# Binary cross-entropy over 8192 x 8192: three slots of predictions with one slot of 8-bit targets, in place of two slots of each

## Chip, cores and metric

The kernel runs on one core of one Trainium2 chip. The metric is the device time of one execution in microseconds (us); for the kernel before it is the median of three runs. Engines are named as in the profile: DVE is VectorE, ACT is ScalarE, POOL is GpSimd, SP is SyncE. DMA transfers are issued from the instruction queues of POOL, SP or ACT and are carried out by the core's 16 DMA engines.

## What is computed

For two float32 arrays of 8192 x 8192 the kernel returns a third of the same shape. `target` holds only 0.0 and 1.0.

```python
pred = np.clip(pred, eps, 1 - eps)          # eps = 1e-7
return -(target * np.log(pred) + (1 - target) * np.log(1 - pred))
```

As a target is 0 or 1, both kernels compute -ln|t - 1 + p|: that is -ln(p) for t = 1 and -ln(1 - p) for t = 0.

## The kernel before, in words

All arrays are read as flat lists. A chunk of w columns is a stretch of 128 x w numbers, and each of the 128 partitions holds w numbers of it that lie together in memory. The whole array is 524,288 columns, and a full chunk is 15,360 columns (60 KiB a partition in float32).

`plan` (L15) lays the chunks out: two halves of 7,680 columns, then 32 full chunks, then two halves and a last piece. `ring_p` (L58) holds predictions in float32, in two slots of 15,360 columns and a small one for the last piece. The result is written over the predictions in place and stored from there. `ring_t` (L59) has the same layout in bfloat16; the load of the targets converts from float32 on the way (L73). A small side piece of 32 rows and 1,408 columns goes through tiles of its own (`side_p`, `side_t`), with four loads or stores of 8 rows each on SP.

Each stretch passes five instructions:

- clip (L92, DVE): max and min with the two bounds
- merge (L95, DVE): (t - 1) + p, which reads the targets
- Abs and Ln (L98, L99, ACT)
- negate (L102, DVE): times -1

The order is written out by hand and each engine keeps it. In the main loop a chunk is worked in two halves of 7,680: clip and merge of the first half, clip and merge of the second, negate of the first, negate of the second. Then the store of the chunk is issued on POOL, and behind it on the same queue the target load and the prediction load of the chunk after next, which go into the same slot:

```python
        for k in range(2, n - 4):
            front(k, (0, 2))
            front(k, (1, 2))
            back(k, (0, 2))
            back(k, (1, 2))
            store(k)
            ...
            for j in range(k + 2, n if k == n - 5 else k + 3):
                load(j)
```

A target slot is free as soon as its merges are done. A prediction slot is free only when the store that reads it has landed, so POOL waits at each prediction load (L74) for the store that it has just issued. At the end the last full chunk is followed by two halves and the last piece, and the last three stores are on SP.

Of the kernel before, what the change touches and what calls it, by code (L numbers as in the profile page):

```python
# [1 line left out]

# [4 lines left out]

EPS = 1e-7

BIG = 15 * 1024  # L10
HALF = BIG // 2
SIDE = 1408


def plan(total):  # L15

    n, last = divmod(total, BIG)
    assert n > 4 and 0 < last <= 2048
    spots = [(HALF, 0), (HALF, HALF)]
    spots += [(BIG, k % 2 * BIG) for k in range(1, n - 1)]  # L20
    end = (n - 1) % 2 * BIG
    return spots + [(HALF, end), (HALF, end + HALF), (last - SIDE // 4, 2 * BIG)]

@with_exitstack
def kernel(
    ctx: ExitStack,
    tc: tile.TileContext,
    pred: bass.AP,  # L30
    target: bass.AP,
    out: bass.AP,
):
    nc = tc.nc
    fp32 = mybir.dt.float32
    bf16 = mybir.dt.bfloat16
    Alu = mybir.AluOpType
    Act = mybir.ActivationFunctionType
    P = nc.NUM_PARTITIONS

    R, C = pred.shape
    spots = plan(R * C // P)
    n = len(spots)
    widths = [w for w, _ in spots]
    turn = n // 2
    cut = R * C - sum(widths[:turn]) * P
    starts = [cut + sum(widths[:k]) * P for k in range(turn)]
    starts += [sum(widths[turn:k]) * P for k in range(turn, n)]

    def chunk(ap, k):  # L50
        flat = ap.rearrange("r c -> (r c)")
        return flat[starts[k] : starts[k] + widths[k] * P].rearrange("(p w) -> p w", p=P)

    pool = ctx.enter_context(tc.tile_pool(name="rings", bufs=1))
    ring = [P, 2 * BIG + widths[-1]]
    ring_p = pool.tile(ring, fp32, name="ring_p", tag="ring_p")
    ring_t = pool.tile(ring, bf16, name="ring_t", tag="ring_t")
    warm = pool.tile([1, 8], fp32, name="warm", tag="warm")  # L58
    side_p = pool.tile([32, SIDE], fp32, name="side_p", tag="side_p")  # L59
    side_t = pool.tile([32, SIDE], fp32, name="side_t", tag="side_t")  # L60

    def side(ap, j):
        flat = ap.rearrange("r c -> (r c)")
        return flat[cut - 32 * SIDE : cut].rearrange("(p w) -> p w", p=32)[j:32:4]

    def spot(ring, k, part=(0, 1)):
        w, c = spots[k]
        i, m = part
        return ring[:, c + i * w // m : c + (i + 1) * w // m]

    def load(k):
        queue = nc.sync if k == 0 else nc.gpsimd
        nc.gpsimd.dma_start(out=spot(ring_t, k), in_=chunk(target, k))  # L73
        queue.dma_start(out=spot(ring_p, k), in_=chunk(pred, k))  # L74

    def store(k):
        queue = nc.sync if k >= n - 3 else nc.gpsimd
        queue.dma_start(out=chunk(out, k), in_=spot(ring_p, k))  # L78

    def load_side():  # L80
        nc.vector.memset(side_p[:, 0:2], 0.5)  # L81
        nc.vector.memset(side_t[:, 0:2], 0.0)  # L82
        for j in range(4):
            nc.sync.dma_start(out=side_t[j:32:4, :], in_=side(target, j))
            nc.sync.dma_start(out=side_p[j:32:4, :], in_=side(pred, j))

    def store_side():
        for j in range(4):
            nc.sync.dma_start(out=side(out, j), in_=side_p[j:32:4, :])

    def front_of(p, t):
        nc.vector.tensor_scalar(  # L92
            out=p, in0=p, scalar1=EPS, scalar2=1 - EPS, op0=Alu.max, op1=Alu.min
        )
        nc.vector.scalar_tensor_tensor(  # L95
            out=p, in0=t, scalar=1.0, in1=p, op0=Alu.subtract, op1=Alu.add
        )
        nc.scalar.activation(out=p, in_=p, func=Act.Abs)  # L98
        nc.scalar.activation(out=p, in_=p, func=Act.Ln)  # L99

    def back_of(p):
        nc.vector.tensor_scalar(out=p, in0=p, scalar1=-1.0, scalar2=None, op0=Alu.mult)  # L102

    def front(k, *part):
        front_of(spot(ring_p, k, *part), spot(ring_t, k, *part))

    def back(k, *part):
        back_of(spot(ring_p, k, *part))

    with tc.manual_schedule():  # L110
        nc.vector.memset(warm, 1.0)  # L111
        for k in range(3):
            load(k)
        nc.scalar.activation(out=warm, in_=warm, func=Act.Ln)  # L114
        front(0)
        front(1)
        back(0)
        store(0)
        back(1)
        store(1)  # L120
        load(3)
        for k in range(2, n - 4):
            front(k, (0, 2))
            front(k, (1, 2))
            back(k, (0, 2))
            back(k, (1, 2))
            store(k)
            if k == n - 6:
                load_side()
            if k == n - 5:  # L130
                front_of(side_p, side_t)
            for j in range(k + 2, n if k == n - 5 else k + 3):
                load(j)
        z, a, b, c = range(n - 4, n)
        front(z, (0, 2))
        back_of(side_p)
        store_side()
        front(z, (1, 2))
        back(z, (0, 2))
        front(a)  # L140
        back(z, (1, 2))
        store(z)
        front(b, (0, 2))
        front(b, (1, 2))
        back(a)
        store(a)
        front(c)
        back(b)
        store(b)
        back(c)  # L150
        store(c)


# [1 line left out]
_INS = ['pred', 'target']  # L155
_OUTS = [((8192, 8192), 'float32')]


# [23 lines left out]
```

## Time and profile before

| what | value |
|---|---|
| runs | 1865.12, 1866.41, 1866.94 us; median 1866.41 |
| span of the profiled execution, first to last instruction | 1864.3 us |
| what lies around the span, against the median of the runs | 2.1 us |
| DVE busy | 1124.7 us (60%) |
| ACT busy | 902.1 us (48%) |
| POOL busy (its DMA issues) | 57.6 us (3%) |
| bytes at the SBUF side of the transfers | 671.22 MB |
| read from HBM, written to HBM | 536.87 MB, 268.44 MB |
| HBM traffic over the span | 432 GB/s |
| merge (L95), 128x7680 | 67 times, 8158 ns each |
| clip (L92) and negate (L102), 128x7680 | 67 and 68 times, 4157 and 4160 ns each |
| Abs (L98) and Ln (L99), 128x7680 | 67 times each, 6596 and 6602 ns |

The profile has no separate time for the execution that it shows: the span stands for it, and what lies around it is taken as the difference to the median. In the page, "busy" is the time in which an engine executes; waits for a semaphore are not in it. The DMA row gives the mean busy share of the 16 DMA engines in 40 slices, and the GB/s row under it counts bytes at the SBUF side, where a target counts 2 bytes before the change although 4 are read from HBM. In a row of the timeline the first two numbers are the start and the duration in us, and the brackets tell how long the engine had been idle and what ended that.

### The profile page before, as it was taken

The numbers are of one execution on the slowest core, as the hardware profiler recorded it, in microseconds if no ns is written. First come the engines' busy times: TensorE is split into PE (matmuls) and PEld (weight loads), VectorE is DVE, ScalarE is ACT, GpSimd is POOL, SyncE is SP. The second block draws the span as 40 slices with busy tenths as digits, with TensorE's granted clock in tenths as the row PEclk, the third lists the DMA queues.
The fourth block names the chain that finished last, engine by engine and source line by source line (L and its number), as shares of the span: only waits on it lengthen the run. The fifth ranks groups of instructions, "written<-read, shape, count | busy, mean of one in ns | idle before, by whom it ended". The sixth has DMA issues, their size and how long they took to land.

```text
span 1864.3 us, 649 instructions
## 1 busy us (share of the span) xinstructions
DVE 1124.7 (60%) x215; ACT 902.1 (48%) x144; POOL 57.6 (3%) x111
## 2 busy tenths in 40 slices
DVE  4655766555676655557665555766555576655585
ACT  3355553335555333555533355553335555333665
POOL 0000000000000000000000000000000000000000
DMA  9999999999999999999999999999999999999999
GB/s 295 376 357 340 357 339 370 386 380 355 341 355 343 369 388 379 356 341 355 349 364 388 380 355 343 353 353 360 389 378 355 349 348 353 359 388 384 347 341 385
DMA packets 16180, 671.22 MB, mean 360 GB/s; under 512 B 1872, under 2 KB 1872, under 8 KB 2352
## 3 DMA queue, kind: packets, MB, share of 16 engines
q0 software_dynamic: 15408, 657.98, 98.4%
q1 hardware_dynamic: 768, 13.21, 1.7%
q14 instruction: 4, 0.03, 0.0%
HBM read 536.87 MB, written 268.44 MB: 432 GB/s over the span
## 4 chain that ended last, share of the span: by engine, by line
DMA 35%; issue 26%; ACT 22%; DVE 15%; POOL 1%; DVEq 0%; POOLq 0%; PEldq 0%
DMA ring_p<-in_pred_dram 32%; ACT ring_p L98 11%; ACT ring_p L99 11%; DVE ring_p L95 7%; DVE ring_p L92 4%; DVE ring_p L102 4%; DMA out_dram<-ring_p 3%; POOL ring_t L73 0%; POOL out_dram L78 0%; DVEq L177 0%; POOL ring_p L74 0%; POOLq L78 0%; POOLq L73 0%; DVEq L92 0%; PEldq L177 0%
## 5 line engine op out<-in xcount | busy, mean ns | idle before, releaser
L98 ACT ACTIVATE ring_p<-ring_p 128x7680 f32<-128x7680 f32 (+1 forms) x70 | 450.3, 6433 | 933.4 <-DVE ring_p L95 933.4
L95 DVE SCALAR_TENSOR_TENSOR ring_p<-ring_t,ring_p 128x7680 f32<-128x7680 bf16 (+1 forms) x70 | 556.9, 7955 | 2.4
L92 DVE TENSOR_SCALAR ring_p<-ring_p 128x7680 f32<-128x7680 f32 (+1 forms) x70 | 283.8, 4055 | 397.9 <-DMA ring_p<-in_pred_dram 397.9
L102 DVE TENSOR_SCALAR ring_p<-ring_p 128x7680 f32<-128x7680 f32 (+1 forms) x69 | 283.8, 4114 | 321.2 <-ACT ring_p L99 321.2
L99 ACT ACTIVATE ring_p<-ring_p 128x7680 f32<-128x7680 f32 (+1 forms) x70 | 450.8, 6440 | 2.2
L74 POOL DMA_DIRECT2D ring_p<-in_pred_dram x36 | 19.3, 536 | 909.5 <-DMA out_dram<-ring_p 909.5
L78 POOL DMA_DIRECT2D out_dram<-ring_p x34 | 18.3, 539 | 852.0 <-DVE ring_p L102 827.7
L73 POOL DMA_DIRECT2D ring_t<-in_target_dram x37 | 20.3, 550 | 0.8 <-PEq L177 0.8
L98 ACT ACTIVATE side_p<-side_p 32x1408 f32<-32x1408 f32 x1 | 1.4, 1375 | 6.7 <-DVE side_p L95 6.7
L114 ACT ACT_TABLE_LOAD x1 | 1.3, 1283 | 0.7 <-PEq L166 0.7
L95 DVE SCALAR_TENSOR_TENSOR side_p<-side_t,side_p 32x1408 f32<-32x1408 f32 x1 | 1.6, 1611 | 0.0
L99 ACT ACTIVATE side_p<-side_p 32x1408 f32<-32x1408 f32 x1 | 1.4, 1375 | 0.0
L92 DVE TENSOR_SCALAR side_p<-side_p 32x1408 f32<-32x1408 f32 x1 | 0.9, 874 | 0.0
L102 DVE TENSOR_SCALAR side_p<-side_p 32x1408 f32<-32x1408 f32 x1 | 0.9, 873 | 0.0
L111 DVE MEMSET warm<- 1x8 f32 x1 | 0.1, 65 | 0.8 <-PEq L166 0.8
L114 ACT ACTIVATE warm<-warm 1x8 f32<-1x8 f32 x1 | 0.2, 208 | 0.0
L166 POOL MEMSET const-float32-0.0<- 128x1 f32 x1 | 0.1, 98 | 0.2 <-issue 0.2
L166 POOL MEMSET const-bfloat16-1.0<- 128x1 bf16 x1 | 0.1, 101 | 0.0
L166 POOL MEMSET const-uint8-127<- 128x1 uint8 x1 | 0.1, 99 | 0.0
L166 POOL MEMSET const-float32-1.0<- 128x1 f32 x1 | 0.1, 98 | 0.0
L81 DVE MEMSET side_p<- 32x2 f32 x1 | 0.1, 60 | 0.0
L82 DVE MEMSET side_t<- 32x2 f32 x1 | 0.1, 60 | 0.0
## 6 DMA issues: line engine op xcount, KB each, us to landing
ring_p<-in_pred_dram POOLq DMA_DIRECT2D x32, 7680.0 KB, 35.9
out_dram<-ring_p POOLq DMA_DIRECT2D x32, 7680.0 KB, 29.2
ring_t<-in_target_dram POOLq DMA_DIRECT2D x32, 3840.0 KB, 46.8
ring_p<-in_pred_dram POOLq DMA_DIRECT2D x3, 3840.0 KB, 35.7
ring_t<-in_target_dram POOLq DMA_DIRECT2D x4, 1920.0 KB, 28.2
out_dram<-ring_p POOLq DMA_DIRECT2D x2, 3840.0 KB, 28.1
out_dram<-ring_p SPq DMA_DIRECT2D x2, 3840.0 KB
ring_p<-in_pred_dram SPq DMA_DIRECT2D x1, 3840.0 KB
```

What stands on the lines that cost most here:

```text
L73: nc.gpsimd.dma_start(out=spot(ring_t, k), in_=chunk(target, k))
L74: queue.dma_start(out=spot(ring_p, k), in_=chunk(pred, k))
L78: queue.dma_start(out=chunk(out, k), in_=spot(ring_p, k))
L81: nc.vector.memset(side_p[:, 0:2], 0.5)
L82: nc.vector.memset(side_t[:, 0:2], 0.0)
L92: nc.vector.tensor_scalar(out=p, in0=p, scalar1=EPS, scalar2=1 - EPS, op0=Alu.max, op1=Alu.min)
L95: nc.vector.scalar_tensor_tensor(out=p, in0=t, scalar=1.0, in1=p, op0=Alu.subtract, op1=Alu.add)
L98: nc.scalar.activation(out=p, in_=p, func=Act.Abs)
L99: nc.scalar.activation(out=p, in_=p, func=Act.Ln)
L102: nc.vector.tensor_scalar(out=p, in0=p, scalar1=-1.0, scalar2=None, op0=Alu.mult)
L114: nc.scalar.activation(out=warm, in_=warm, func=Act.Ln)
L166: nc = _bacc.Bacc("TRN2", target_bir_lowering=False, num_devices=1)
```

## The change

- **Slots.** `ring_p` has three slots of 15,360 columns. `ring_t` has one slot of 15,360 columns in uint8, so the target load converts float32 to 8-bit integers and the merge reads 8-bit integers.
- **Chunks.** The first chunk has 5,120 columns, then come 33 full chunks, then a tail of 5,632, 5,632 and 1,024 columns that together lie in one slot. The stretches follow each other in memory from the start. The side piece and its tiles are gone.
- **Order on POOL.** In the loop: the target load of the next chunk (it waits for the merges of this chunk), the store of this chunk (it waits for the negates), the prediction load of the chunk after next (it waits for the store of the chunk before, whose slot it takes). The very first prediction load is on ACT's queue.
- **Order on DVE.** merge, merge, negate, negate of chunk k, then clip, clip of chunk k+1. Before, the clips came right ahead of the merges of their own chunk.
- **End.** The three tail predictions are loaded behind the store of chunk 32, the three tail targets behind the merges of chunk 33. DVE then has negate of the first half of chunk 33, the three tail clips, the first tail merge, and only then negate of the second half of chunk 33 and its store. The last four stores are on SP; the very last is cut into 108, 12 and 8 rows.

```diff
-    spots = [(HALF, 0), (HALF, HALF)]
-    spots += [(BIG, k % 2 * BIG) for k in range(1, n - 1)]
-    end = (n - 1) % 2 * BIG
-    return spots + [(HALF, end), (HALF, end + HALF), (last - SIDE // 4, 2 * BIG)]
+WIDE = 15360
+SLOTS = 3
+TAIL = (5632, 5632, 1024)
+ROWS = (108, 12, 8)
...
+    low = mybir.dt.uint8
...
+    spots = [(first, 0)]
+    spots += [(WIDE, k % SLOTS * WIDE) for k in range(1, n + 1)]
+    c = (n + 1) % SLOTS * WIDE
+    for w in TAIL:
+        spots.append((w, c))
+        c += w
...
-    ring_p = pool.tile(ring, fp32, name="ring_p", tag="ring_p")
-    ring_t = pool.tile(ring, bf16, name="ring_t", tag="ring_t")
+    ring_p = pool.tile([P, SLOTS * WIDE], fp32, name="ring_p", tag="ring_p")
+    ring_t = pool.tile([P, WIDE], low, name="ring_t", tag="ring_t")
...
-    def load(k):
-        queue = nc.sync if k == 0 else nc.gpsimd
-        nc.gpsimd.dma_start(out=spot(ring_t, k), in_=chunk(target, k))
-        queue.dma_start(out=spot(ring_p, k), in_=chunk(pred, k))
+    def load_p(k):
+        queue = nc.scalar if k == 0 else nc.gpsimd
+        queue.dma_start(out=p_of(k), in_=chunk(pred, k))
+
+    def load_t(k):
+        nc.gpsimd.dma_start(out=t_of(k), in_=chunk(target, k))
 
     def store(k):
-        queue = nc.sync if k >= n - 3 else nc.gpsimd
-        queue.dma_start(out=chunk(out, k), in_=spot(ring_p, k))
+        queue = nc.sync if k >= z else nc.gpsimd
+        r = 0
+        for rows in ROWS if k == n - 1 else (P,):
+            queue.dma_start(out=chunk(out, k)[r : r + rows, :], in_=p_of(k)[r : r + rows, :])
+            r += rows
...
+    halves = (0, 2), (1, 2)
+    tail = range(z + 1, n)
     with tc.manual_schedule():
+        load_p(0)
+        load_t(0)
+        load_p(1)
...
+        for h in halves:
+            clip(0, h)
+        for k in range(z):
+            for h in halves:
+                merge(k, h)
+            load_t(k + 1)
+            for h in halves:
+                negate(k, h)
+            for h in halves:
+                clip(k + 1, h)
             store(k)
+            for j in (k + 2,) if k + 2 <= z else tail if k + 2 == z + 1 else ():
+                load_p(j)
+        for h in halves:
+            merge(z, h)
+        for j in tail:
+            load_t(j)
+        negate(z, halves[0])
+        for j in tail:
+            clip(j)
+        merge(z + 1)
+        negate(z, halves[1])
         store(z)
+        merge(z + 2)
+        negate(z + 1)
+        store(z + 1)
+        merge(z + 3)
+        negate(z + 2)
+        store(z + 2)
+        negate(z + 3)
+        store(z + 3)
```

In the changed kernel `merge` holds the merge, Abs and Ln of a stretch, `clip` and `negate` one instruction each. z is 33, the last full chunk, and the tail is chunks 34, 35 and 36.

## The prediction

> **What bounds the kernel now.** I read the page first (busy shares, the DMA row, HBM bytes), then the timeline for the clips (each waits for a prediction load, so its start is a landing time), then one period of the loop, then the windows view.
>
> ```profile
> DVE 1124.7 (60%) x215; ACT 902.1 (48%) x144; POOL 57.6 (3%) x111
> ...
> DMA  9999999999999999999999999999999999999999
> ...
> HBM read 536.87 MB, written 268.44 MB: 432 GB/s over the span
> ```
>
> No engine is busy for more than 60%, while the DMA engines are in the top tenth in every slice. POOL's 909.5 us of waiting and ACT's 933.4 are waits of engines that have time. The kernel is as long as its transfers.
>
> ```profile
> 590.00:600.00 10.00, 8.62 (x2) 10.00 (x2) 0.00 (x0) 1.00 1.08 233
> ...
> 674.00:690.00 16.00, 11.40 (x2) 0.00 (x0) 0.00 (x0) 1.00 1.02 442
> ```
>
> The last two numbers are the DMA share and GB/s at the SBUF side. The first stretch is a target load, the second a prediction load. Both keep the DMA engines full, but the target load lands half as much a microsecond: the time goes by the 4 bytes read per number, not by the 2 that land.
>
> ```profile
> 40.29 4.16 DVE L92 TENSOR_SCALAR ring_p<-ring_p 128x7680 f32<-128x7680 f32 x1 [8.14 <-DMA ring_p<-in_pred_dram]
> ...
> 78.15 4.16 DVE L92 TENSOR_SCALAR ring_p<-ring_p 128x7680 f32<-128x7680 f32 x1 [8.04 <-DMA ring_p<-in_pred_dram]
> ...
> 406.83 4.16 DVE L92 TENSOR_SCALAR ring_p<-ring_p 128x7680 f32<-128x7680 f32 x1 [12.31 <-DMA ring_p<-in_pred_dram]
> ...
> 515.50 4.16 DVE L92 TENSOR_SCALAR ring_p<-ring_p 128x7680 f32<-128x7680 f32 x1 [11.38 <-DMA ring_p<-in_pred_dram]
> ...
> 1711.11 4.16 DVE L92 TENSOR_SCALAR ring_p<-ring_p 128x7680 f32<-128x7680 f32 x1 [11.42 <-DMA ring_p<-in_pred_dram]
> ```
>
> From 515.50 to 1711.11 lie 22 chunks of three transfers, 66 in all: **18.115 us for one transfer of 15,360 columns** (a unit). By 40.29 two units are through (four halves): 36.2 us of work, so the landing is 4.1 late. By 78.15 it is 4 units, late by 5.7; by 406.83 22 units, late by 8.3; by 515.50 28 units, again late by 8.3. So the lateness grows by 4.2 us in the first 400 us and then stands still. The views do not tell why it grows.
>
> **The change, part by part.** Bytes at HBM are the same: three times 524,288 columns, 102.4 units, 1855.0 us. What can change is the lateness, stalls in which no transfer is queued, and the end.
>
> *8-bit targets.* The load still reads 4 bytes per number. By the two window rows its time goes by those, so I cost it at 0. The trace shows no 8-bit load: as bounds, 2% less of a unit (more would contradict rows in which half the bytes landed brought nothing) is -0.36 x 33.3 targets = -12 us, and 2% more +12. The merge reads 8-bit where it read bfloat16. The rows have 1611 ns for 1,408 columns of float32 targets and 1926 for 1,696 of bfloat16: about 1.14 ns a column in both, so the type of the targets does not show, and I take 0. If it took twice as long, see the rivals.
>
> *The loop.* Call T the landing of targets k. The queue then holds store k-1, predictions k+1, targets k+1: busy until T + 54.3. Here are the distances from a merge to its store, before:
>
> ```profile
> 411.02 8.16 DVE L95 SCALAR_TENSOR_TENSOR ring_p<-ring_t,ring_p 128x7680 f32<-128x7680 bf16 x1
> ...
> 438.98 6.60 ACT L99 ACTIVATE ring_p<-ring_p 128x7680 f32<-128x7680 f32 x1
> 445.62 4.16 DVE L102 TENSOR_SCALAR ring_p<-ring_p 128x7680 f32<-128x7680 f32 x1 [8.97 <-ACT ring_p L99]
> 450.07 0.54 POOL L78 DMA_DIRECT2D out_dram<-ring_p  x1 [24.33 <-DVE ring_p L102]
> ```
>
> From the first merge to the store's issue it is 39.05 us; ACT's four passes make it, so a merge pair without a clip between changes nothing. In the changed loop the merges end at T + 16.4 and targets k+1 are issued then, 20 us before the queue reaches them (T + 36.2). Store k is issued at T + 39.05, 15 us before T + 54.3. Predictions k+2 wait for store k-1, landed at T + 18.1, and go out right behind store k. DVE needs 2 x 8.16 + 2 x 4.16 + 2 x 4.16 = 33.0 of 54.3 us. The single target slot is thus hidden by two queued transfers, and the loop stays at 54.35 us a chunk. Cost 0.
>
> *The first chunk is short*, and there the cover is thin. When targets 1 land (2.67 units), the queue holds store 0 (a third), predictions 2 and targets 2: until T + 42.3. Store 1 goes out at T + 39.05 and moves data 1.1 later (a store issued on POOL at 1819.64 shows in the windows from 1820: 241 GB/s, then 538), at T + 40.2. That is 2.1 us of cover. But clip 2 now starts on DVE 0.3 us before that issue, where before DVE waited at this place. One spot of the trace has a DVE clip over a POOL issue:
>
> ```profile
> 1753.98 0.87 DVE L92 TENSOR_SCALAR side_p<-side_p 32x1408 f32<-32x1408 f32 x1
> 1754.35 0.62 POOL L78 DMA_DIRECT2D out_dram<-ring_p  x1 [24.32 <-DVE ring_p L102]
> 1754.88 1.61 DVE L95 SCALAR_TENSOR_TENSOR side_p<-side_t,side_p 32x1408 f32<-32x1408 f32 x1
> 1754.97 0.55 POOL L73 DMA_DIRECT2D ring_t<-in_target_dram  x1
> ```
>
> The issue takes 0.62 us in place of 0.54 (mean 539 ns over 34) and ends 0.12 after the clip. I read it as: an issue under a clip is held until the clip ends. With a clip of 4.16 the data of store 1 start at T + 38.8 + 4.16 + 0.12 + 0.8 = T + 43.9, a stall of **1.6 us**, once. From below it is 0 (no hold), from above 5.8 (held through both clips). In the loop the same hold, at worst to T + 48.1, is covered by T + 54.3. The Trainium skill says the same of this spot (SBUF — State Buffer, section "SBUF: two separate sides"): while VectorE runs an operation that takes both ports, GpSimd cannot write the descriptors of the transfers that it issues. By that rule the sum is the forecast or up to 4.2 us above it; without it, 1.6 below. The 0.12 us agree with it, on one short row.
>
> *Lateness.* The same traffic, now each store between a target load and a prediction load. Bounds: 4.1 (no growth after the first 40 us) and 8.7 (the last clip before the end, 1765.70 after 97 units, is 8.5 late). I take the 8.3 that the rows hold from 407 us on. The first load moves from SP's queue to ACT's: both engines are free at 0.7 us, cost 0.
>
> *The end.* T is now the landing of targets 33: 98 units are through. T = 1775.3 + 8.3 + 1.6 = 1785.2. The queue still holds store 32 and the tail's loads (0.8 + 0.8 units), until T + 47.1. DVE: merges to T + 16.4; negate of the first half when Ln is done, T + 21.6 to 25.8; clips 34 and 35 (3.1 each, from the rows for 7,680 and 3,840 columns) and 36 follow their loads and end at T + 35.2. Merge 34 waits for targets 34 (T + 39.3) and takes 6.0; negate of the second half of chunk 33 stands behind it and ends at T + 49.5; store 33 moves data 1.1 later, T + 50.6. **A gap of 3.5 us** in which no transfer is queued. Before, the store of the last full chunk was issued at 1819.64, about when the last loads ended, and the windows dip to a share of 0.89 for a microsecond. Bounds for the gap: 2.5 to 5 (the issue delay, and loads that end earlier on some DMA engines). Stores 34, 35 and 36 are ready at T + 59, 68 and 69, before the queue reaches them (T + 68.7, 75.3, 82.0): covered. The cut of the last store into three: between 0 and 1.2 us (its 1,024 columns are 1.2 us if spread evenly), I take 0.5. From T on: 4.4 units = 79.7, gap 3.5, cut 0.5, closing 1.0 (the same sum of before leaves 2.0 from 97 units to the span's end, about 1 of it that dip): 84.7.
>
> *Sum.* 1785.2 + 84.7 = 1869.9 span. Against the 1864.3 of before that is +5.6, of which the gap makes 3.5, the stall 1.6, the cut 0.5. With the 2.1 us around the span: **1872.0 us**, +0.30% on the median 1866.41, if the run shown is like the others (they lie within 1.8 us).
>
> **Rivals.**
>
> - *No hold* (an issue under a clip is not delayed): 1870.4. For it: the held row is a single one, and short. At +0.21% it lies on the edge of what a measurement tells from no change, which I take as 0.2%, or 3.7 us.
> - *The long hold*, through both clips: 1876.2. The clips stand 0.04 us apart, so the issue may not slip in between.
> - *The lateness stays small*, 4.1 to 6.5 in place of 8.3, because the traffic is mixed in another way: 1866.2 to 1868.6 without the hold. Nothing in the trace ties its growth to the order, so it may not return.
> - *Faster: the 8-bit load is shorter.* Its place is each of the 33 target loads. It decides from 0.28 us a load (9.3 us in all, to pass the forecast's +5.6 and 3.7 beyond); at 2% of a unit it gives 1872.0 - 12 = 1860.0. Against it: the window rows.
> - *The 8-bit merge at half speed.* Merges to T + 32.6, Ln to 45.8, negate to 50, clips to 58.3: the loop would be bound by DVE and ACT at 58.3, +4 us in each of 32 chunks, about 2000. Against it: the two rows of the side piece and the last piece.
>
> **How the numbers follow.** Chances: forecast 0.36, long hold 0.12, no hold 0.20, small lateness 0.18, shorter 8-bit load 0.09, slow 8-bit merge or load 0.05. Faster by over 0.2% (under 1862.7) is the shorter load alone: 0.09. Within 0.2% are the small lateness and nearly half of no hold: 0.27. Slower (over 1870.1) is the rest: 0.64. The range reaches from the low end of the small lateness to just above the long hold: 1866 to 1877. Outside lie the two 8-bit cases.
>
> **What would show it.** The loop: clips 54.35 us apart from 500 us on; any other distance refutes the 8-bit cost. The hold: POOL store issues longer than 0.54 us where a clip runs, and a dip of the DMA share near 95 us. The end: DMA share under 0.5 for some 3 us between the last load and store 33, whose issue follows merge 34 and a negate. The lateness: the start of the merges against units of 18.115. The forecast is wrong if the gap is not there, or if T lies before 1782.

## The result, and the profile after

| | before | changed |
|---|---|---|
| median of 5 runs, us | 1866.53 (1865.12 to 1867.57) | 1877.67 (1876.93 to 1880.62) |
| ratio | | 1.0064, 95% interval 1.0052 to 1.0075 |
| span of the profiled execution, us | 1864.3 | 1876.2 (its time: 1878.45) |

The change makes the kernel 0.64% slower, 11.1 us. Forecast were +5.6 us and 1872.0; 1877.67 lies just above the range (1866 to 1877). (In the description of the kernel before, the tiles `ring_p` and `ring_t` are at L56 and L57.)

First the page of the changed kernel: the totals, the DMA row, the HBM bytes, and POOL's groups (count, then busy us and mean ns of one issue, then idle time before).

```profile
DVE 1116.7 (60%) x214; ACT 900.3 (48%) x144; POOL 277.6 (15%) x110
...
DMA  9999999999999999999999999999999999999998
...
HBM read 536.87 MB, written 268.44 MB: 429 GB/s over the span
...
L79 POOL DMA_DIRECT2D out_dram<-ring_p x33 | 125.1, 3791 | 711.5 <-DVE ring_p L99 711.5
L73 POOL DMA_DIRECT2D ring_t<-in_target_dram x37 | 19.7, 532 | 818.8 <-DVE ring_p L91 818.1
L70 POOL DMA_DIRECT2D ring_p<-in_pred_dram x36 | 132.9, 3692 | 0.0
```

HBM traffic is the same and the DMA row is still full but for the last slice. New is POOL: its store issues take 3,791 ns in place of 539 and its prediction issues 3,692 in place of 536. Its busy time of 277.6 us is waiting in disguise: only the two kinds of issue that come where a clip runs are long; the target issues, which come where DVE waits (once under a merge), stay at 532.

The timeline of the changed kernel at the first full chunk, and the DMA share there (next to last number):

```profile
93.49 8.23 DVE L85 TENSOR_SCALAR ring_p<-ring_p 128x7680 f32<-128x7680 f32 x2
93.87 3.89 POOL L79 DMA_DIRECT2D out_dram<-ring_p  x1 [21.99 <-DVE ring_p L99]
97.76 4.09 POOL L70 DMA_DIRECT2D ring_p<-in_pred_dram  x1
```

```profile
95.00:96.00 1.00, 1.00 (x1) 0.00 (x0) 1.00 (x1) 1.00 0.00 0
96.00:97.00 1.00, 1.00 (x1) 0.00 (x0) 1.00 (x1) 1.00 0.00 0
97.00:98.00 1.00, 1.00 (x2) 0.00 (x0) 1.00 (x2) 1.00 0.00 0
98.00:99.00 1.00, 1.00 (x1) 0.00 (x0) 1.00 (x1) 1.00 2.31 983
```

The store's issue ends 0.12 us after the first of the two clips, the load's issue 0.12 us after the second. The DMA share is counted where a packet starts: none starts for some three microseconds, then all DMA engines start at once. By the trace's packet records no packet was in flight from 96.71 to 98.33, a stall of 1.6 us. The store then landed 3.0 us late: its last packets took 2.8 to 3.4 us on all 16 engines, in place of 2.27.

Now the lateness, read at the merges (each waits for its targets). In the changed order targets k are transfer 3k - 1, so the chunks below are units 8, 56 and 98:

```profile
155.36 16.23 DVE L91 SCALAR_TENSOR_TENSOR ring_p<-ring_t,ring_p 128x7680 f32<-128x7680 uint8 x2 [6.84 <-DMA ring_t<-in_target_dram]
...
1029.62 16.23 DVE L91 SCALAR_TENSOR_TENSOR ring_p<-ring_t,ring_p 128x7680 f32<-128x7680 uint8 x2 [7.41 <-DMA ring_t<-in_target_dram]
...
1790.51 16.23 DVE L91 SCALAR_TENSOR_TENSOR ring_p<-ring_t,ring_p 128x7680 f32<-128x7680 uint8 x2 [7.48 <-DMA ring_t<-in_target_dram]
```

With 18.115 us a unit they are late by 10.4, 15.2 and 15.2 us (chunks 3, 19 and 33). From 1029.62 to 1790.51 lie 14 chunks, 54.35 us each, as before. So the loop itself costs nothing; the lateness does, and it is made before 1030 us.

The end, in the timeline and the windows:

```profile
1829.85 6.02 DVE L91 SCALAR_TENSOR_TENSOR ring_p<-ring_t,ring_p 128x5632 f32<-128x5632 uint8 x1 [4.20 <-DMA ring_t<-in_target_dram]
1835.80 4.15 DVE L99 TENSOR_SCALAR ring_p<-ring_p 128x7680 f32<-128x7680 f32 x1
...
1839.98 0.40 SPq L79 DMA_DIRECT2D out_dram<-ring_p  x1
```

```profile
1838.00:1839.00 1.00, 1.00 (x1) 1.00 (x1) 0.00 (x0) 1.00 0.00 0
1839.00:1840.00 1.00, 1.00 (x2) 1.00 (x1) 0.00 (x0) 1.00 0.00 0
1840.00:1841.00 1.00, 1.00 (x1) 0.97 (x2) 0.00 (x0) 1.00 2.16 922
```

This is the forecast gap: merge, negate, store on SP, with the loads over. No packet was in flight from 1837.40 to 1840.87, 3.5 us (the expectations below put it at 3.9).

**Where the 11.9 us of span went.** In the kernel before, the store of chunk 32 ends 98 units. POOL's next load waits for it:

```profile
1784.27 0.54 POOL L74 DMA_DIRECT2D ring_p<-in_pred_dram  x1 [28.76 <-DMA out_dram<-ring_p]
```

The store's last completion mark lies 0.28 us earlier, at 1784.0, late by 8.7. The changed kernel is there at 1790.5, late by 15.2: 6.5 us. From there to the end it is 80.3 before and 85.7 now: 5.4 us.

### The profile page after: what moved, and what is told of

Same layout as the page of the kernel before. It is cut to its first block, busy times and chain, and to the rows that moved or that the text cites. A ratio compares the mean times of both kernels' runs of the same rounds, so it can differ in the third digit from the quotient of the medians.

```text
span 1876.2 us, 663 instructions
## 1 busy us (share of the span) xinstructions
DVE 1116.7 (60%) x214; ACT 900.3 (48%) x144; POOL 277.6 (15%) x110
## 4 chain that ended last, share of the span: by engine, by line
DMA 67%; issue 28%; DVE 2%; ACT 2%; POOL 0%; POOLq 0%; DVEq 0%; PEldq 0%
DMA ring_t<-in_target_dram 67%; DVE ring_p L91 2%; ACT ring_p L95 1%; ACT ring_p L94 1%; DVE ring_p L99 0%; POOL ring_p L70 0%; POOL out_dram L79 0%; DVEq L165 0%; POOLq L73 0%; POOLq L79 0%; DVEq L91 0%; PEldq L165 0%
## 5 line engine op out<-in xcount | busy, mean ns | idle before, releaser
L94 ACT ACTIVATE ring_p<-ring_p 128x7680 f32<-128x7680 f32 (+3 forms) x71 | 450.8, 6349 | 954.1 <-DVE ring_p L91 954.1
L91 DVE SCALAR_TENSOR_TENSOR ring_p<-ring_t,ring_p 128x7680 f32<-128x7680 uint8 (+3 forms) x71 | 554.3, 7846 | 251.4 <-DMA ring_t<-in_target_dram 251.4
L99 DVE TENSOR_SCALAR ring_p<-ring_p 128x7680 f32<-128x7680 f32 (+3 forms) x71 | 284.3, 4006 | 470.6 <-ACT ring_p L95 470.6
L95 ACT ACTIVATE ring_p<-ring_p 128x7680 f32<-128x7680 f32 (+3 forms) x71 | 451.3, 6356 | 2.3
L85 DVE TENSOR_SCALAR ring_p<-ring_p 128x7680 f32<-128x7680 f32 (+3 forms) x71 | 281.3, 4003 | 19.9 <-DMA ring_p<-in_pred_dram 19.9
L79 POOL DMA_DIRECT2D out_dram<-ring_p x33 | 125.1, 3791 | 711.5 <-DVE ring_p L99 711.5
L70 POOL DMA_DIRECT2D ring_p<-in_pred_dram x36 | 132.9, 3692 | 0.0
```

The lines of the kernel that those rows point to most:

```text
L70: queue.dma_start(out=p_of(k), in_=chunk(pred, k))
L79: queue.dma_start(out=chunk(out, k)[r : r + rows, :], in_=p_of(k)[r : r + rows, :])
L85: nc.vector.tensor_scalar(out=p, in0=p, scalar1=EPS, scalar2=1 - EPS, op0=Alu.max, op1=Alu.min)
L91: nc.vector.scalar_tensor_tensor(out=p, in0=t, scalar=1.0, in1=p, op0=Alu.subtract, op1=Alu.add)
```

## The experiments

The theory: three costs. POOL issues are *held* under a clip, which stalls the transfers once, near 95 us; that stall puts the 16 DMA engines in step, and the lateness then grows anew (*start again*); and there is the *gap* at the end. Rivals: the order of transfers or the 8-bit type makes the lateness grow; the hold or the gap costs nothing. All ratios are against the kernel before, run on the same chip.

### e1: no clip under a POOL issue

```diff
+            pause()
             for h in halves:
                 clip(k + 1, h)
```

`pause` is one scalar_tensor_tensor of 128x1536 on a spare tile, 1.75 us.

> A merge-type operation of 128x1536 on a spare tile (about 1.8 us, and DVE has 21 us to spare per chunk) stands on DVE between the negates of a chunk and the clips of the next, so that the store and the prediction load of POOL are issued before a clip runs. Theory 'hold': POOL issues take 0.54 us again, the stall of 3 us near 95 us is gone, and as the DMA engines are not put in step again by it, part of the later growth of the lateness (10.4 at chunk 3 to 15.2 at chunk 33) goes as well: 1871 to 1873 us. Rival 'order': the growth comes from every store now standing behind an 8-bit target load, so only the stall goes: about 1874.7. Rival 'hold does not matter': 1877 to 1878.

Measured: 1873.66 us, 1.0039 (1.0027 to 1.0052). The timeline at the same place:

```profile
92.95 1.75 DVE L99 SCALAR_TENSOR_TENSOR spare<-spare 128x1536 f32<-128x1536 f32 x1
93.33 0.54 POOL L80 DMA_DIRECT2D out_dram<-ring_p  x1 [22.00 <-DVE ring_p L105]
93.85 0.53 POOL L71 DMA_DIRECT2D ring_p<-in_pred_dram  x1
94.61 8.22 DVE L86 TENSOR_SCALAR ring_p<-ring_p 128x7680 f32<-128x7680 f32 x2
```

More work on DVE makes the kernel 4.0 us faster: the hold is shown. It is not every DVE instruction that holds: the store's issue runs its 0.54 us under the spare operation. The lateness is 8.1 at chunk 3 and 10.7 at chunk 33, against 10.4 and 15.2:

```profile
153.07 16.23 DVE L92 SCALAR_TENSOR_TENSOR ring_p<-ring_t,ring_p 128x7680 f32<-128x7680 uint8 x2 [1.77 <-DMA ring_t<-in_target_dram]
...
1785.94 16.23 DVE L92 SCALAR_TENSOR_TENSOR ring_p<-ring_t,ring_p 128x7680 f32<-128x7680 uint8 x2 [5.68 <-DMA ring_t<-in_target_dram]
```

So 2.3 us are gone by chunk 3 and another 2.3 in the growth behind it. The time lies between the two theories' numbers.

### e2: the store of chunk 33 earlier, on SP

```diff
-        merge(z + 1)
         negate(z, halves[1])
         store(z)
+        merge(z + 1)
         merge(z + 2)
```

> The second negate of chunk 33 and its store stand ahead of the first tail merge on DVE; nothing else changes. Theory 'gap': the last full store is issued about 8 us before the loads end, the 3.9 us gap goes, and with it about 3.9 us: 1873 to 1874. Rival 'the gap is only moved': the tail's later stores are then late, or the end is set by the slowest DMA engine that had no gap: 1876 to 1878.

Measured: 1877.70 us, 1.0062 (1.0048 to 1.0075): nothing gained. The rival holds. The store went out at 1829.24, with loads of the tail still queued on POOL. The second tail merge then waited for its targets (the bracket gives the wait):

```profile
1845.20 6.03 DVE L91 SCALAR_TENSOR_TENSOR ring_p<-ring_t,ring_p 128x5632 f32<-128x5632 uint8 x1 [9.75 <-DMA ring_t<-in_target_dram]
```

Those targets took 15.8 us from the ones before them (1829.4 to 1845.2) in place of 6.6. Transfers of two queues are served side by side, so the early store took a share of the rate from the loads that the end waits for, and the gap moved to where the later stores were not ready: no packet was in flight for 3.1 us from 1862.0, and the DMA share is 0.65 over the last 15 us. The Trainium skill says so of the queues (DMA: Bandwidth & Descriptors, section "Queues, rings and completion order"): each DMA engine takes the queues in turn, packet by packet. The trace agrees: a load of 6.6 us became 2.4 times as long.

### e3: the kernel before with 8-bit targets

```diff
-    bf16 = mybir.dt.bfloat16
+    bf16 = mybir.dt.uint8
```

> The kernel before with targets in 8 bits in place of bfloat16, all else the same. Theory 'the type is free': within 1 us of before, 1865.5 to 1867.5, and the lateness of a clip at 515 us is again about 8.3 us. Rival 'type': 8-bit loads make the changes between loads and stores dearer, lateness grows beyond 8.3, some 1869 to 1872.

Measured: 1866.70 us, 1.0003 (0.9994 to 1.0011); the clip at 514.86 is late by 7.6. The type is free, for the load and for the merge.

### e4: all stores on SP

```diff
-        queue = nc.sync if k >= z else nc.gpsimd
+        queue = nc.sync
```

> All stores on SP's queue in place of POOL's; the loads stay on POOL. Stores cannot be held under a clip, and they are mixed with loads in another way, since two queues are served side by side. Theory 'hold': no stall near 95 us, at least 3 us less, 1871 to 1875. Theory 'order': as a store no longer starts on all DMA engines where a target load ends, the lateness grows less: down to 1868. Rival 'neither': 1877 or more, for example if a prediction load now overtakes and a store lands late.

Measured: 1930.73 us, 1.0349 (1.0335 to 1.0363), 53 us slower than the changed kernel. Both theories have the time wrong. The rival 'neither' holds, though it put no number on how far above 1877. The hold is gone (POOL busy 55.3 us), but stores and loads now share the rate, loads land later than the order supposes, and the single target slot is refilled too late. One such place in the windows and the timeline:

```profile
685.00:690.00 5.00, 5.00 (x1) 4.97 (x2) 0.00 (x0) 1.00 0.34 147
690.00:695.00 5.00, 1.29 (x1) 5.00 (x1) 1.06 (x2) 1.00 0.62 83
```

```profile
675.06 16.23 DVE L91 SCALAR_TENSOR_TENSOR ring_p<-ring_t,ring_p 128x7680 f32<-128x7680 uint8 x2 [25.70 <-DMA ring_t<-in_target_dram]
...
691.59 0.53 POOL L73 DMA_DIRECT2D ring_t<-in_target_dram  x1 [50.24 <-DVE ring_p L91]
```

DVE had waited 25.7 us for these targets (7 in the changed kernel), and until the merges end at 691.3 the next target load cannot be issued: for some 6 us little moves. The Trainium skill's advice for a held issue (SBUF — State Buffer, section "Summary: rules for kernel authors") is to issue the transfer from ACT or SP. It does end the hold here; in this kernel the measured price of a second queue is thirteen times the hold's.

### e5: the store of chunk 33 earlier, on POOL

```diff
-        queue = nc.sync if k >= z else nc.gpsimd
+        queue = nc.sync if k > z else nc.gpsimd
```
and the order of e2.

> As e2 (second negate of chunk 33 and its store ahead of the first tail merge), but this store is issued on POOL, behind the tail's loads in the same queue. Theory: in e2 the store on SP's queue was served side by side with the tail's last loads and held them back (5,632 targets took 15.8 us in place of 6.6), so the gap only moved; in one queue the loads go first, the gap of 3.9 us goes and nothing is late: 1873 to 1874.5. Rival: the end is bound by the slowest DMA engine or by the tail's compute, 1876 to 1878.

Measured: 1872.65 us, 1.0035 (1.0022 to 1.0047), 5.0 us less than the changed kernel. In one queue the store waits behind the loads, and the second tail merge starts at 1836.81, 46.0 us after targets 33 (in e2 it was 55.1). From targets 33 to the end it is 81.2 us in place of 85.7. The gap is shown. Taking it away brought more than the time in which nothing moved, and the run lies 0.35 us below the range of the theory.

### e6: targets, predictions, store

```diff
-            store(k)
             for j in (k + 2,) if k + 2 <= z else tail if k + 2 == z + 1 else ():
                 load_p(j)
+            store(k)
```

> In the loop the prediction load of chunk k+2 is issued ahead of the store of chunk k in place of behind it (targets, predictions, store); DVE, ACT and the tail as in the changed kernel. The first iteration then has a whole prediction transfer more in the queue, so the hold under a clip (still seen as issues of some 4 us) is covered and the stall goes. Theory 'order' (a store that starts behind a target load costs more at each start than one behind a prediction load): lateness at chunk 33 falls from 15.2 to 8 or 9 us, 1870.5 to 1872. Rival 'start again' (only the stall, which puts the DMA engines in step, makes the extra growth): lateness as in e1, 10.6 us, 1873 to 1874.5. Rival 'the hold is not covered': 1877.

Measured: 1874.85 us, 1.0042 (1.0030 to 1.0055). Store issues still take 3.7 us, yet there is no stall, as a whole prediction transfer more is queued. The lateness at chunk 33 is 11.5: not the 8 to 9 of 'order'. That theory falls: with and without a target load ahead of the store, the versions without stall (e1, e6 to e9) end late by 10.1 to 11.5, those with it by 14.8 to 15.6 (changed kernel 15.2, e2 14.8, e5 15.6, e11 15.0). The exception is e12, below.

### e7 and e8: both repairs together

e7 is e6 and e5, e8 is e1 and e5; no further edit.

> e6 and e5 together. If the two costs are separate they add: 3.9 us below e6, 1866.5 to 1868 by 'order', 1869 to 1870.5 by 'start again'.

> e1 and e5 together (a spare operation on DVE ahead of the clips, and the store of chunk 33 on POOL ahead of the tail's merges). If the two costs are separate they add: 1873.7 - 3.9 = 1869.8, 1869 to 1871. If one hides the other, 1872 to 1874.

Measured: e7 1868.53 us, 1.0009 (1.0000 to 1.0018); e8 1868.38 us, 1.0011 (1.0002 to 1.0020). e7 is 6.3 below e6 and e8 5.3 below e1: the two costs are separate, and the gap is worth 5.0 to 6.3 where 3.9 was expected. Taking away the stall brings 4.0 (e1), 2.8 (e6), 4.3 (e8 against e5) and 4.1 (e7 against e5). Together they are some 9.2 of the 11.1 us.

### e9: the addresses in the old order

```diff
-    starts = [sum(w for w, _ in spots[:k]) * P for k in range(n)]
+    turn = n // 2
+    cut = sum(w for w, _ in spots[turn:]) * P
+    starts = [cut + sum(w for w, _ in spots[:k]) * P for k in range(turn)]
+    starts += [sum(w for w, _ in spots[turn:k]) * P for k in range(turn, n)]
```
on e7.

> e7 (targets, predictions, store; store of chunk 33 on POOL ahead of the tail's merges) with the addresses in the order of the kernel before: the first half of the chunks is the upper part of the arrays, the second half the lower. Theory 'addresses': the 1.5 to 2 us of lateness that e7 still has over the kernel before (10.2 against 8.5 at the last chunk) go: 1866 to 1867. Rival 'addresses do not matter': as e7, 1868 to 1869.

Measured: 1867.99 us, 1.0008 (0.9999 to 1.0016), lateness 10.7 at chunk 33. Not told from e7: the addresses don't explain the rest.

### e10: one late store in the kernel before

```diff
+            if k == 16:
+                for _ in range(20):
+                    nc.vector.scalar_tensor_tensor(...)
             back(k, (1, 2))
             store(k)
```

> The kernel before with 20 spare operations of 1.2 us on DVE ahead of the second negate of chunk 16, so that this one store goes out some 24 us later than Ln would allow, when the queue has been empty for 5 to 6 us on the slowest DMA engine (the last predictions land 11 us after a store's usual issue, the store goes out 15.5 later than usual and needs 0.8 to move data). Theory 'start again': the lateness of the clips, 8.3 us before, jumps by about 5.5 and then grows by another 1.5 to 3 us as it does at the start of the kernel: 1873.5 to 1875.5. Rival 'a stall costs itself': it jumps and stays: 1871.5 to 1872.5.

Measured: 1883.00 us, 1.0089 (1.0075 to 1.0102), above both numbers, because the edit made a hold as well. With the negate late, the next clip stood right behind it:

```profile
900.75 4.15 DVE L93 TENSOR_SCALAR ring_p<-ring_p 128x7680 f32<-128x7680 f32 x1
901.13 3.89 POOL L79 DMA_DIRECT2D out_dram<-ring_p  x1 [40.35 <-DVE ring_p L103]
```

The stall, taken by landings, was therefore 11.0 us (the store landed 65.35 after the store before it, 860.24 to 925.59 on POOL, in place of 54.35), with no packet in flight for 9.8 us of it. What tells the theories apart is what comes behind it, the clips at units 46, 52, 70 and 94:

```profile
841.87 4.16 DVE L93 TENSOR_SCALAR ring_p<-ring_p 128x7680 f32<-128x7680 f32 x1 [11.44 <-DMA ring_p<-in_pred_dram]
...
962.50 4.16 DVE L93 TENSOR_SCALAR ring_p<-ring_p 128x7680 f32<-128x7680 f32 x1 [18.82 <-DMA ring_p<-in_pred_dram]
...
1292.69 4.16 DVE L93 TENSOR_SCALAR ring_p<-ring_p 128x7680 f32<-128x7680 f32 x1 [12.25 <-DMA ring_p<-in_pred_dram]
...
1728.08 4.16 DVE L93 TENSOR_SCALAR ring_p<-ring_p 128x7680 f32<-128x7680 f32 x1 [11.42 <-DMA ring_p<-in_pred_dram]
```

They are late by 8.6, 20.5, 24.6 and 25.3 us. The jump is 11.9; then, in a lateness that had stood still for 300 us, another 4.1 us are lost in six chunks, and 0.7 in the eight behind them. 'Start again' is shown, in that the lateness grows anew behind a stall: this one cost 16.3 us.

### e11: the last store in one piece

```diff
-ROWS = (108, 12, 8)
+ROWS = (128,)
```

> The changed kernel with the last store of 1,024 columns in one piece in place of 108, 12 and 8 rows. Estimate on record: the cut costs 0.5 us (between 0 and 1.2): 1877.2, which is inside the spread of the runs; the time from the landing of targets 33 to the end of the span, 85.7 us in the changed kernel, would be 85.2. Rival: the cut costs nothing or gains.

Measured: 1877.32 us, 1.0057 (1.0044 to 1.0071). From the merge of chunk 33 (1790.30) to the end (1874.9) it is 84.6 us in place of 85.7: the cut costs about 1.1 us in the profile, the upper of its bounds. In the times that does not show.

### e12: e7 without held issues

The pause of e1 on e7.

> e7 with the spare operation of e1 ahead of the clips, so that no POOL issue is held. Theory: in e7 the hold is covered by the queue in every iteration, so it costs nothing and the time stays, 1868 to 1869, though the issues go from 3.6 us back to 0.54. Rival 'held issues also slow the transfers': 1866 to 1867.

Measured: 1867.75 us, 1.0010 (1.0001 to 1.0019), as e7. A hold that the queue covers costs nothing that could be measured. Its profiled execution was the longest of its eleven (1871.4), with a lateness of 14.6 at chunk 33 and no stall: the executions of this one kernel lie up to 4.5 us apart (from 1866.95), so a single profile weighs little in a question of 1 or 2.

## Why the prediction was wrong

It was right that the time would go up, in every place that it named, and wrong in the size: 1869.9 for the span against 1876.2.

- **8-bit targets at no cost**: right (e3).
- **The loop at 54.35 us a chunk**: right, to the hundredth, from 1030 us on.
- **The hold and the stall of 1.6 us**: right, read from a single issue that took 0.62 in place of 0.54 us. The issue ended 0.12 after the clip, as there, and no packet was in flight for 1.6 us. The cover was sized right too: targets 2 were to land 42.3 us after targets 1 and did after 42.2 (by the trace's completion marks). The Trainium skill says (SBUF — State Buffer, section "SBUF: two separate sides") that GpSimd cannot write the descriptors of its transfers while VectorE holds the ports that they share. The trace agrees: all 32 held stores end 0.12 us after the clip, and e1 ends the hold.
- **The lateness of 8.3 us: this is the step that failed.** The sum took it from the rows of the kernel before and added the stall to it, as if the two stood for themselves. In place of 8.3 + 1.6 = 9.9 it was 15.2: 5.3 of the 6.3 us that the sum lacks. e1 splits them, by one profile each. Without the stall the lateness is 10.7 there, so 4.5 us come with the stall: 1.6 of standing still, and 2.9 of growth behind it, which the sum had at nothing. e10 shows such growth behind a stall in the kernel before. The other 2.4 (10.7 for 8.3) come without any stall, and their cause is open. e6 to e9 lie near e1, at 10.1 to 11.5. The prediction said that the views did not tell why the lateness grows, yet gave it bounds up to 8.7 only, and a rival on the low side only. An unknown growth should have had its upper bound from doing it twice: 8.3 + 4.2.
- **The gap of 3.5 us**: right in place, cause and length. Taking it away brought 5.0 (e5).
- **The cut of the last store, 0.5**: 1.1 (e11). The end took 85.7 against 84.7, and this is 0.6 of the difference.
- **The rivals**: the long hold had the nearest time, 1876.2, but the runs show the short one (one clip for each issue). That the range reached up to 1877, close to the measured time, was owed to a rival that did not happen: luck. A small lateness did not come.

**How it starts again, as far as the trace goes.** Each transfer leaves 16 completion marks, and it is complete with the last. In the changed kernel they lie 2.5 us apart for targets 2, 0.6 for store 1 behind the stall, and 3.7 from 1000 us on; in e10 4.4 before its stall, 0.6 behind it, and 4.1 at the end. While they are close, transfers take up to 19 us in place of 18.1 where loads change to stores; when they are far apart that stops (not in e12, whose last mark loses another 2.4 us from chunk 19 to chunk 33 with the marks 8 to 10 apart). The packets show it too: the last packet of targets 3 took 2.8 to 3.7 us on all 16 engines in place of 2.28; at 370 us nine engines still had one over 0.1 us longer, and from 1000 us on there is hardly any. From the store behind the stall to targets 33 the last mark loses 5.8 us and the first 2.6 (in e10 5.7 and 2.3): a little under half of the growth is time that every mark loses, the rest is the marks moving apart again. Why a change costs more in step was not tried and stays open.

The same marks after 98 units, in us:

| | last mark late by | first mark late by | apart |
|---|---|---|---|
| before | 8.7 | 4.1 | 4.7 |
| changed, with the stall | 15.2 | 11.4 | 3.7 |
| e1 | 10.6 | 6.3 | 4.3 |
| e6 | 11.4 | 4.7 | 6.7 |
| e7 | 10.1 | 3.9 | 6.2 |
| e12 | 14.5 | 4.0 | 10.5 |

With the stall even the first mark is late (10.1 to 11.5 in e2, e5 and e11); without it (e1, e6 to e9, e12) it is 3.9 to 6.3 late, and 4.1 in the kernel before. So e12's large lateness is of another kind than the changed kernel's: its marks lie far apart.

**What stays open too:** e7, e8, e9 and e12 are still 1.1 to 2.0 us slower than the kernel before. Neither the type (e3) nor the addresses (e9) nor the hold (e12) explains it. In e7, e9 and e12 the first mark is as early as before, and only the last is later; what moves the marks farther apart in that order was not tried. No version here beats the kernel before.

## What to carry to other kernels

When the transfers are the bound, look for the one place where the queue runs short, the first iterations and the tail, and check there what stands on every engine between the last wait and the issue: here a clip of 4.2 us that started 0.4 us ahead of a POOL issue held it to the clip's end. Count a stall at more than the time in which nothing moves: here 1.6 us cost 2.8 to 4.3, and 9.8 us cost 16.3. An earlier store gains only if it stays behind the loads in their queue: on a second queue it takes their rate (e2, e4).

## What the runs showed of the hardware that was not expected

- A store of 60 KiB a partition, issued on a second queue beside the tail's loads, made a 6.6 us load take 15.8 (e2), and all stores on SP cost 53 us (e4), at the same bytes.
- The lateness of a saturated DMA queue is no constant: in the kernel before it grew by 4.2 us in the first 400 us and then stood still at 8.3, and in the changed one it grew by 4.8 from chunk 3 to chunk 19 behind the stall and then stood still at 15.2 for 760 us.
- A target load's issue on POOL and the store's issue in e1 ran their usual 0.53 and 0.54 us under a DVE scalar_tensor_tensor, while each of 64 issues under a clip (tensor_scalar) ended 0.12 us behind it.
